# Gate rows by transposes in place of fp32 products with the identity: a hybrid pooling and attention backbone on one core

## The chip, the core and the metric

The kernel runs on one core of a Trainium2 chip. The engines that matter are TensorE (PE in the profile; PEld is its weight load), VectorE (DVE), ScalarE (ACT), GpSimd (POOL) and SyncE (SP), which issues the DMAs. TensorE multiplies a stationary operand, which is loaded first, with a moving operand, and writes the result to PSUM. A transpose on TensorE is an instruction of the same form with its transpose flag set, with the data as one operand and the identity as the other.

The metric is device time in microseconds. Three timed runs of the kernel before gave 1163.19 to 1163.43 us, median 1163.33 us. The execution that was profiled took 1161.48 us.

## The reference

Two layers work on 512 latent tokens and 256 context tokens of 1024 channels, in fp32. The first layer mixes tokens by pooling over windows, the second by attention, and each is followed by a squared-ReLU MLP. Each sub-layer is normalised, shifted and scaled before, and multiplied by a gate after:

```python
for i in range(DEPTH):
    sh1, sc1, gt1, sh2, sc2, gt2 = ada_mods(c, w_ada[i], b_ada[i])
    csh1, csc1, cgt1, csh2, csc2, cgt2 = ada_mods(c_ctx, w_ada[i], b_ada[i])
    h_lat = modulate(rms_norm(x, g_mix_pre[i]), sh1, sc1)
    h_ctx = modulate(rms_norm(ctx, g_mix_pre[i]), csh1, csc1)
    ...
    x = x + gt1 * rms_norm(y_lat, g_mix_post[i])
    ...
    x = x + gt2 * rms_norm(m_lat, g_mlp_post[i])
```

The gate has one value per channel, the product of `gt1` (or `gt2`) and the gain of the norm behind it. The context tokens have gates of their own (`cgt1`, `cgt2`) in the first layer.

## The kernel before

Tokens lie in six tiles of 128 rows (0 to 3 latent, 4 and 5 context). Large products run in fp32r: operands are split into a high and a low part, and three products (high with high, high with low, low with high) are summed in PSUM. ACT makes the high part, DVE the low one.

Conditioning: `ada_mm` multiplies the two conditioning vectors with weights that come by DMA in loads of 1 MB (tile `raw`, result `psada`). `ada_rows`, `ada_sel` and `ada_mods` turn the result into columns: channel k*128 + p lies in partition p, column k of `mods`. The shift and scale of a channel are used in that form.

The gate is needed as a row instead: it multiplies tiles with tokens in the partitions and channels along the free axis, and so has to stand in every partition. `gate_cols` (L317) makes the column form `gc` on DVE. `gate_half` (L326) makes 512 channels of the row form in a PSUM tile `psg`: for each of four columns of `gc` it takes the column, repeated 128 times by a zero stride, as the stationary operand and the identity as the moving one. The result has the column's 128 values along the free axis, the same in each partition. ACT then copies the tile to `gate` in SBUF, and DVE uses it in `gated` (L361). `gate_rows` (L334) calls `gate_half` twice and makes the copies; `gate_diag` (L341) is another way to the same rows, used at three other places, which the change doesn't touch.

`gate_half` runs in two places:

- First stage. Its steps are a list written by hand (`FIRST`), and the instructions of PE, DVE and ACT are kept in that order (class `Kept`; such instructions appear under line 87). The steps `psg:1:0`, `psg:0:0`, `psg:1:1` and `psg:0:1` are four calls (context and latent tokens, two halves of the channels). The copies are the steps `gate:`, the multiplies the steps `b:`, the residuals `r:`; between them stand the pooling products (`pool:`, tile `pspool`), the conditioning products for the MLP (`mm:SC2_0a` and on), their rows, selections and columns (`rows:`, `sel:`, `mods:`), and after them the transposes of the normalised rows (`turn:`, function `turn0`, tile `psx`) and the first products of the MLP (`in:`, tile `psin`).
- Attention. `gate_rows` for GT1 of layer 1 is given a due time between the last product of the probabilities with the values (`s_values`, L1378, tile `po`) and the output products (`attn_mm`, L1403, tile `psy`), whose results `gated` multiplies. The transposes of the probabilities are those of `s_turn` (L1359, tile `pspt`).

Outside the first stage the order is a planner's. Steps are sorted by due times; the framework then simulates the program (option `schedule_with_timeline_sim`) and orders each engine's instructions by that order and by when they are ready. Some instructions are pinned (`keep_in_program_order`). SP issues the DMAs in order; a load waits until its buffer is free.

The first MLP computes its inner products in rounds of seven chains of twelve products (`Seven.chain`, L732), between which ACT copies partial sums (L740, L744); `ada_sum` (L296 to L305) does the remaining conditioning on DVE meanwhile. After the attention output, `norm_pair`, `half_early` and `upper_half` (L1472) prepare the second MLP, whose first products are at L608.

Of the kernel before, what the change touches and what calls it, by code (L numbers as in the profile page):

```python
# [17 lines left out]
P = 128  # L18
# [72 lines left out]
def backbone(ctx: ExitStack, tc, x, ctx_in, w_ada, w_pool, pool_scale, w_qkv, g_q, g_k, w_o, w_mlp_in,  # L91
# [4 lines left out]
    te, ve, sc = Kept(tc, nc.tensor, ordered), Kept(tc, nc.vector, mixed), Kept(tc, nc.scalar, mixed)  # L96
# [20 lines left out]
    ident = const.tile([P, P], F32, name="ident")  # L117
# [208 lines left out]
    def gate_half(ci, h):  # L326
        ps = psB.tile([P, 512], F32, tag="b", name="psg")
        gc = halfgate.pop((ci, h))
        for k in range(4):
            te.matmul(ps[:, k * P:(k + 1) * P], gc[:, 4 * h + k:4 * h + k + 1].broadcast_to([P, P]), ident,  # L330
                      start=True, stop=True)
        halfgate[ci, h] = ps

    def gate_rows(i, m, ci):  # L334
        gc = gate_cols(i, m, ci)
        for h in range(2):
            halfgate[ci, h] = gc
            gate_half(ci, h)
            sc.copy(gate[:, ci, 512 * h:512 * h + 512], halfgate.pop((ci, h)))
# [80 lines left out]
    def mod0(t, q, on_act):  # L420
        ci, ps = 0 if t < NL else 1, turned[t, q]
        for kk in range(2):
            k = 2 * q + kk
            sa, b = avec[0][1][:, k, ci:ci + 1], mods[0][:, SH2 * KT + k, ci:ci + 1]
            h, src = accv[:, t:t + 2, k * P:(k + 1) * P], ps[:, kk, :].rearrange("p (u n) -> p u n", n=P)
            if on_act:
                sc.activation(h, src, AF.Identity, scale=sa, bias=b)
            else:
                ve.tensor_scalar(out=h, in0=src, scalar1=sa, scalar2=b, op0=ALU.mult, op1=ALU.add)
        ks = slice(2 * q, 2 * q + 2)  # L430
        h = accv[:, t:t + 2, 2 * q * P:(2 * q + 2) * P].rearrange("p u (k n) -> p k u n", n=P)
        turned[t, q] = (h, *(z.rearrange("p k (h q n) -> p k q h n", h=2, n=P)[:, ks, t // 2] for z in (hH, hL)))
# [380 lines left out]
    def halved(t, q, part):  # L813
        h, hi, lo = turned[t, q]
        if part:
            ve.tensor_tensor(out=lo, in0=h, in1=hi, op=ALU.subtract)
        else:
            sc.copy(hi, h)

    def keep(store, key, fn, *args):  # L820
        store[key] = fn(*args)
# [5 lines left out]
        sel=lambda x: conditioning(ada_sel, x), mods=lambda x: conditioning(ada_mods, x),  # L827
        hi=lambda k: centred(k, 0), lo=lambda k: centred(k, 1), pool=pool_a,
        gc=lambda ci, h: keep(halfgate, (ci, h), gate_cols, 0, GT1, ci, 4 * h, 4 * h + 4), psg=gate_half,
        gate=lambda ci, h: sc.copy(gate[:, ci, 512 * h:512 * h + 512], halfgate.pop((ci, h))),  # L830
        ms=pool_ms, rs=lambda t: keep(rs, t, rstd, rs[t], 2 if t in (4, 1) else 1),
# [5 lines left out]
        h=lambda t, act, q: mod0(t, q, act), xhi=lambda t, q: halved(t, q, 0), xlo=lambda t, q: halved(t, q, 1))  # L837
# [749 lines left out]
```

## Time and profile before

| | before |
|---|---|
| timed runs, median of 3 | 1163.33 us |
| profiled execution | 1161.48 us |
| its span, first to last instruction | 1159.7 us |
| PE busy, instructions | 1140.7 us (98%), 6172 |
| DVE busy | 932.7 us (80%) |
| ACT busy | 628.8 us (54%) |
| mean granted TensorE clock | 0.999 |

The span is 1.78 us shorter than the execution's time; the rest lies before the first and after the last instruction. Matmuls are pipelined, so that the time of one from start to end is longer than the distance between two; the chain of waits counts each only for the time that it holds up the next. In the chain a row gives start, length, engine, tile, line and count of instructions. In the timeline a bracket gives the idle time of the engine ahead of a group and what ended it.

### The profile page before, as it was taken

The numbers are of one execution on the slowest core, as the hardware profiler recorded it, in microseconds if no ns is written. First come the engines' busy times: TensorE is split into PE (matmuls) and PEld (weight loads), VectorE is DVE, ScalarE is ACT, GpSimd is POOL, SyncE is SP. The second block draws the span as 40 slices with busy tenths as digits, with TensorE's granted clock in tenths as the row PEclk, the third lists the DMA queues.
The fourth block names the chain that finished last, engine by engine and source line by source line (L and its number), as shares of the span: only waits on it lengthen the run. The fifth ranks groups of instructions, "written<-read, shape, count | busy, mean of one in ns | idle before, by whom it ended". The sixth has DMA issues, their size and how long they took to land.

```text
span 1159.7 us, 15945 instructions
## 1 busy us (share of the span) xinstructions
PE 1140.7 (98%) x6172; PEld 990.7 (85%) x6172; DVE 932.7 (80%) x1515; ACT 628.8 (54%) x1068; POOL 69.2 (6%) x120
## 2 busy tenths in 40 slices
PE   7999999999999999999999999999999999999997
PEld 5679889998898988998888889998988888888886
DVE  4688588998988997996777699867687679778876
ACT  5676555554354534555675367753676436534522
POOL 2130000000000000000242200001100000000001
PEclk9999999999999999999999999999999999999999
DMA  9964222443334444343422102125334214313212
GB/s 374 418 270 151 73 99 87 146 145 131 123 145 146 146 146 145 109 146 109 182 73 73 37 1 74 37 74 168 122 146 146 81 64 146 109 44 138 109 41 104
DMA packets 25516, 147.32 MB, mean 127 GB/s; under 512 B 2785, under 2 KB 5217, under 8 KB 9698
## 3 DMA queue, kind: packets, MB, share of 16 engines
q1 hardware_dynamic: 25442, 146.32, 34.4%
q8 instruction: 48, 0.79, 0.3%
q14 instruction: 26, 0.21, 0.1%
HBM read 138.96 MB, written 7.34 MB: 126 GB/s over the span
## 4 chain that ended last, share of the span: by engine, by line
PE 62%; issue 30%; DVE 2%; POOL 2%; ACT 2%; DMA 1%; POOLq 0%; SPq 0%; DVEq 0%; ACTq 0%
PE pso L878 22%; PE psin L732 18%; PE psy L1403 3%; PE po L1378 3%; PE pss L1337 3%; PE psq L1133 2%; PE pspt L1359 2%; PE pspool L87 2%; PE psin L87 1%; PE psin L608 1%; PE psada L87 1%; DMA raw<-in_w_ada 1%; PE psm L87 1%; POOL rs L211 1%; PE psg L87 1%
## 5 line engine op out<-in xcount | busy, mean ns | idle before, releaser
L878 PE MATMUL pso<-units,rb 128*128 128x512 f32 x1152 | 278.8, 392 | 0.0
L878 PEld LDWEIGHTS pso<-units,rb 128*128 128x128 f32 x1152 | 214.7, 188 | 41.1
L301 DVE SCALAR_TENSOR_TENSOR rows<-raw,cond,rows 128x256 f32<-128x256 f32 x280 | 127.2, 478 | 2.0
L890 DVE TENSOR_TENSOR acc<-acc,pso 128x512 f32<-128x512 f32 x129 | 85.4, 676 | 40.5 <-PE pso L878 40.3
L608 PE MATMUL psin<-ra,rb 128*128 128x512 f32 (+1 forms) x310 | 87.8, 360 | 0.0
L987 PE MATMUL pso<-units,pairs 128*128 128x512 f32 x336 | 82.6, 389 | 0.0
L608 PE MATMUL psin<-ra 128*128 128x512 f32 (+1 forms) x256 | 76.5, 376 | 0.0
L987 PEld LDWEIGHTS pso<-units,pairs 128*128 128x128 f32 x336 | 63.1, 188 | 13.1
L991 DVE TENSOR_TENSOR acc<-acc,pso 128x512 f32<-128x512 f32 x72 | 48.7, 682 | 26.2 <-PE pso L987 26.2
L732 PE MATMUL psin<-ra,units 128*128 128x384 f32 x336 | 65.6, 337 | 0.4 <-ACT psin L744 0.4
L209 POOL TENSOR_SCALAR ms<-ss 128x1 f32<-128x1 f32 x16 | 8.7, 541 | 936.6 <-ACT junk L196 922.9
L732 PE MATMUL psin<-sums,units 128*128 128x384 f32 x336 | 64.0, 336 | 0.0
L732 PEld LDWEIGHTS psin<-ra,units 128*128 128x128 f32 x336 | 59.9, 188 | 3.9 <-ACT psin L744 0.5
L608 PEld LDWEIGHTS psin<-ra,rb 128*128 128x128 f32 x310 | 55.6, 189 | 8.7
L169 DVE TENSOR_TENSOR units<-raw,units 128x1024 fp32r<-128x1024 f32 (+2 forms) x49 | 55.1, 1152 | 8.6 <-ACT units L166 8.4
L732 PEld LDWEIGHTS psin<-sums,units 128*128 128x128 f32 x336 | 58.9, 188 | 1.6
L608 PE MATMUL psin<-rb 128*128 128x512 f32 (+1 forms) x155 | 55.8, 361 | 0.6 <-DVE rb L1472 0.6
L166 ACT CAST units<-raw 128x1024 fp32r<-128x1024 f32 (+2 forms) x49 | 46.9, 996 | 17.0 <-PE pso L878 12.9
L608 PEld LDWEIGHTS psin<-ra 128*128 128x128 f32 x256 | 47.1, 188 | 8.8
L888 ACT COPY acc<-pso 128x512 f32<-128x512 f32 x48 | 27.1, 586 | 46.9 <-PE pso L878 46.4
L1133 PE MATMUL psq<-units,ra 128*128 128x512 f32 x216 | 52.2, 393 | 0.0
L608 PE MATMUL psin<-rb,ra 128*128 128x512 f32 (+1 forms) x128 | 48.1, 376 | 0.0
(284 smaller groups left out, 2385.5 us busy)
## 6 DMA issues: line engine op xcount, KB each, us to landing
raw<-in_w_ada SPq DMA_DIRECT2D x48, 1024.0 KB, 5.2
raw<-in_w_mlp_in SPq DMA_DIRECT2D x32, 1024.0 KB, 4.9
raw<-in_w_mlp_out SPq DMA_DIRECT2D x32, 1024.0 KB, 5.8
raw<-in_w_qkv SPq DMA_DIRECT2D x6, 1024.0 KB, 4.9
spill<-xr SPq DMA_DIRECT2D x10, 512.0 KB, 4.3
xr<-spill SPq DMA_DIRECT2D x10, 512.0 KB, 6.7
raw<-in_w_o SPq DMA_DIRECT2D x4, 1024.0 KB, 4.8
xr<-in_x SPq DMA_DIRECT2D x4, 512.0 KB, 5.3
```

The source lines that it names most:

```text
L87: return lambda *args, **kw: self.tc.keep_in_program_order(f(*args, **kw))
L166: a = sc.copy(hi, raw)
L169: b = ve.tensor_tensor(out=lo, in0=raw, in1=hi, op=ALU.subtract)
L301: ve.scalar_tensor_tensor(out=r, in0=raw[:, k, :], scalar=cond[:, k, c:c + 1], in1=r, op0=ALU.mult, op1=ALU.add)
L608: te.matmul(ps[:, bank, o:o + ln], w[:, k, fs], rhs, start=start, stop=(k == KT - 1 and n == 2), skip_group_check=len(ks) < KT or self.paired)
L732: te.matmul(bank, w[k], a[k], start=start and k == 0 and m == 0, stop=stop and k == 3 and m == 2, skip_group_check=True)
L878: te.matmul(pss[h][:, 0:cols[h][1]], a[:, f, ts_], w[:, f, cols[h][0]:sum(cols[h])], start=(n == 0 and not seeded[t]), stop=(n == len(seq) ...
L890: ve.tensor_tensor(out=d, in0=d, in1=ps[:, 0:w], op=ALU.add)
L987: te.matmul(ps, a, w, start=(m == 0), stop=(m == len(seq) - 1))
L991: ve.tensor_tensor(out=M[n][:, t], in0=M[n][:, t], in1=ps, op=ALU.add)
L1133: te.matmul(ps, a[:, k, sl], w[:, k % 4, :], start=(k == 0 and n == 0), stop=(k == KT - 1 and n == 2))
L1337: te.matmul(ps[:, c2, 0:384], a[:, sl], b[:, kv, 384 * c2:384 * c2 + 384], start=(n == 0), stop=(n == 2))
```

## The change

`gate_half` calls the transpose in place of the product; operands, tile, count of calls and what waits for them stay as they are.

```diff
         ps = psB.tile([P, 512], F32, tag="b", name="psg")
         gc = halfgate.pop((ci, h))
         for k in range(4):
-            te.matmul(ps[:, k * P:(k + 1) * P], gc[:, 4 * h + k:4 * h + k + 1].broadcast_to([P, P]), ident,
-                      start=True, stop=True)
+            te.transpose(ps[:, k * P:(k + 1) * P], gc[:, 4 * h + k:4 * h + k + 1].broadcast_to([P, P]), ident)
         halfgate[ci, h] = ps
```

## The prediction

> **What bounds the kernel.** I read the page first, then the chain of waits around the two places where gate rows are made, then what each engine waited for there.
>
> ```profile
> span 1159.7 us, 15945 instructions
> PE 1140.7 (98%) x6172; PEld 990.7 (85%) x6172; DVE 932.7 (80%) x1515; ACT 628.8 (54%) x1068; POOL 69.2 (6%) x120
> PEclk9999999999999999999999999999999999999999
> ```
>
> TensorE (PE) is busy for 1140.7 of 1159.7 us at full clock, so work that leaves PE is worth its time if nothing else ends last in its stage. That has to be seen stage by stage. The chain through the first place (start, length, what):
>
> ```profile
> 46.64 0.91 PE pspool L87 x6
> 47.55 0.89 PE psg L87 x8
> 48.44 1.00 PE psada L87 x8
> 49.44 1.09 PE psg L87 x8
> ...
> 52.32 0.89 PE psg L87 x8
> 53.21 0.71 PE pspool L87 x6
> 53.93 0.89 PE psg L87 x8
> ...
> 67.45 0.87 PE psx L87 x8
> 68.33 0.22 PE psada L87 x13
> ```
>
> and a window over the same stretch (length, busy time of each engine, clock, DMA share, GB/s):
>
> ```profile
> 47.39:68.55 21.16, 21.16 (x190) 15.91 (x188) 14.08 (x18) 15.44 (x28) 9.41 (x16) 1.00 1.01 418
> ```
>
> Between 47.4 and 68.5 us the chain lies on PE without a break: 21.16 us busy of 21.16. The four gate halves (psg) stand in that chain, so PE ends last there. DMA is full as well (share 1.01), and has to be examined below. The second place, in the attention:
>
> ```profile
> 769.57 0.22 PE psg L330 x2
> 769.79 1.07 PE po L1378 x9
> 770.86 1.56 PE psg L330 x14
> 772.42 38.12 PE psy L1403 x168
> ```
>
> Again PE goes from the last value products (po) through psg into 38 us of output products (psy) with no gap.
>
> **What one half costs now and then.** A half is four products of 128x128, one per 128 channels.
>
> ```profile
> L87 PE MATMUL psg<-ident,gc x32: 270/275/376, 47.4 to 54.5; 128*128 128x128 f32 x32
> L330 PE MATMUL psg<-ident,gc x16: 270/275/275, 769.4 to 772.1; 128*128 128x128 f32 x16
> ```
>
> Sixteen calls of the first stage leave 32 records and eight calls of the attention leave 16: a full fp32 product is two passes. The 275 ns is a latency; what a call takes of the pipe is read from the chain: 0.89 / 8 = 0.111 us per pass. One half shows 1.09 instead of 0.89; the 0.20 more is its start behind the narrow psada products, and I leave it in place. Transposes in this kernel, timeline and then chain:
>
> ```profile
> 86.10 1.91 PE L87 MATMUL psx<-ident,acc 128*128 128x128 f32 x16
> ```
>
> ```profile
> 72.98 1.02 PE psx L87 x8
> ...
> 86.26 1.75 PE psx L87 x16
> ```
>
> Sixteen calls (one group of turn0 is four calls, and four groups run here) leave sixteen records: a fp32 transpose is one pass, of 1.75 / 16 = 0.109 us. Where a group starts behind psada, as in the row at 72.98, it is 1.02 / 8 = 0.128 with the start included.
>
> **The sum.** Before: 0.89 + 1.09 + 0.89 + 0.89 = 3.76 us in the first stage and 0.22 + 1.56 = 1.78 us in the attention, 5.54 in all. After: 16 x 0.109 + 0.20 = 1.94 and 8 x 0.109 = 0.87, 2.81 in all. Gain 1.82 + 0.91 = 2.73 us.
>
> No row has a transpose whose data operand repeats one column (zero stride), so its price is bounded. From below by 0.109, since no transpose row is faster; from above by 2 x 0.111 = 0.222, what the same operand costs in the full product, at which the gain is nothing. With 0.128 for all 24 the gain is 5.54 - 3.07 = 2.47. I take 0.109, since the present psg passes, with the same repeated column, keep 0.111 against 0.109 and so show no sign that the stride matters. Nothing is added elsewhere: same tiles, same PSUM buffers, same copies to the gate, no DMA, no new wait.
>
> The Trainium skill, page "TensorE: Matmul & The Clock Gate", section "Terms", calls the transpose mode four times faster for FP32. By that a half would be 0.89 / 4 = 0.22 us and the gain 4.0 us, an estimate from that page. The trace has one record in place of two and 0.109 against 0.111 per record, so a factor of two; the sum goes by the trace.
>
> **What is late next, first stage.** The instructions of that stage keep the order of the list FIRST on PE, DVE and ACT, so nothing is reordered there; PE's steps after the fourth half come 1.8 us earlier if their inputs do. Three streams could hold them back.
>
> DMA: eight loads of conditioning weights go out from 34.67 us on, in the order SC2_0a, SC2_0b, SH2_0a and so on. The second, issued at 37.41, is the tightest:
>
> ```profile
> 37.41 0.33 SPq L147 DMA_DIRECT2D raw<-in_w_ada  x1
> ```
>
> ```profile
> raw<-in_w_ada SPq DMA_DIRECT2D x1, 1024.0 KB, 16.5
> ```
>
> ```profile
> 55.46 1.07 PE L87 MATMUL psada<-raw,cond 128*32 128x512 f32 x8
> ...
> 57.36 1.06 PE L87 MATMUL psada<-raw,cond 128*32 128x512 f32 x8
> ```
>
> It lands at 37.41 + 16.5 = 53.9 and is used at 57.36, so there are 3.4 us, and 1.6 remain after a shift of 1.8. DMA is full but ahead.
>
> ACT and DVE, and a window over DVE's longest run (DVE is the third busy time):
>
> ```profile
> 53.25 0.59 ACT L87 COPY gate<-psg 128x512 f32<-128x512 f32 x1 [1.16 <-PE psg L87]
> ...
> 69.11 1.02 ACT L87 ACTIVATE acc<-psx,mods,avec 128x256 f32<-128x256 f32 x2 [2.61 <-DVE mods L87]
> ```
>
> ```profile
> 53.87 1.23 DVE L87 TENSOR_TENSOR acc<-acc,gate 128x1024 f32<-128x1024 f32 x1 [0.21 <-ACT gate L87]
> ...
> 65.17 0.72 DVE L87 STREAM_TRANSPOSE work<-psada 128x512 f32<-128x512 f32 x1 [0.96 <-PE psada L87]
> 68.57 0.17 DVE L87 TENSOR_TENSOR mods<-psada,vec 128x8 f32<-128x8 f32 x1 [2.68 <-PE psada L87]
> ```
>
> ```profile
> 53.87:64.22 10.35, 10.35 (x85) 7.27 (x87) 9.93 (x10) 8.75 (x16) 6.85 (x10) 1.00 1.01 419
> ```
>
> DVE is busy for 9.93 of the 10.35 us from 53.87 to 64.22, the rest being the steps between instructions, and that run starts when the third half's gate copy ends. The copy can come 3 x 0.45 us earlier, but DVE's own work in front of the run ended only 0.21 us before it and moves by the two halves ahead of it, 0.9: the run moves by 0.9 + 0.2 = 1.1 us, not 1.8. The missing 0.7 us is covered: DVE waits for PE 0.96 us at 65.17 and 2.68 us at 68.57, and ACT waits 2.61 us at 69.11. With that idle gone the price would be 0.7. So the whole 1.8 us arrives at 68.5, where DVE and ACT start the next stage from PE's result, and everything behind, its DMAs included, moves by the same amount.
>
> **Attention.** The eight calls stand between po and psy. The gate copies that follow (ACT) serve the multiply at 778.0, which waits for psy anyway. Later waits:
>
> ```profile
> 778.01 0.69 DVE L361 TENSOR_TENSOR acc<-psy,gate 128x512 f32<-128x512 f32 x1 [0.49 <-PE psy L1403]
> ...
> 810.58 0.69 DVE L361 TENSOR_TENSOR acc<-psy,gate 128x512 f32<-128x512 f32 x1 [1.74 <-PE psy L1403]
> ```
>
> ```profile
> 822.84 0.39 PE L608 MATMUL psin<-rb 128*128 128x256 f32 x1 [0.61 <-DVE rb L1472]
> ```
>
> At 778 DVE has 0.49 us of idle, less than 0.91, so its filler work moves less than PE; by 810.58 it has 1.74 us in hand, and that covers it. PE's only wait there, 0.61 us for the lower half's split, hangs on DVE and ACT steps that start from the last psy product, and moves along. If DVE's cover were gone, 0.4 us of the 0.91 would be.
>
> **Forecast.** Profiled execution: 1161.48 us, span 1159.70 and 1.78 around it. Span after 1159.70 - 2.73 = 1156.97, that execution 1158.75. The median of the timed runs is 1.85 us above the profiled one; the same 2.73 off it gives 1163.33 - 2.73 = 1160.6 us, a gain of 0.23%. What a measurement can tell from no change is 0.2%, 2.33 us, so this clears it by 0.4 us only.
>
> **Rivals.**
>
> 1. Half is hidden. Another stream takes over in the first stage and only the attention's 0.91 counts: 1162.4. For it: DMA at 1.01 and DVE without idle for ten microseconds. Against: 1.6 us of slack on the tightest load, 2.68 us of DVE idle before 68.57.
>
> 2. A new plan makes it slower. Outside the first stage most instructions are not pinned; their order comes from a planner that simulates the program, and a shorter psg can change it. Place: the products of the first MLP (L732) and the copy of their partial sum (L744), behind the changed stage. PE waited for that copy once (the 0.4 behind the last bar):
>
> ```profile
> L732 PE MATMUL psin<-ra,units 128*128 128x384 f32 x336 | 65.6, 337 | 0.4 <-ACT psin L744 0.4
> ```
>
> A round has two such chains of twelve, so the 336 records are fourteen rounds. If ACT ran a cast ahead of that copy in every round, 14 x 0.4 = 5.6 us are lost and 2.73 gained: 1166.2. It decides from seven rounds on (2.73 / 0.4). For it: the same loop body is planned anew each round, and ACT has casts ready beside the copy. Against: behind 68.5 us all streams move alike, so the planner sees the same relative times there. A smaller slip, one to six rounds, only eats into the gain: 1161 to 1163.
>
> 3. The repeated column makes the transpose slow, above 0.222 us a call. At four passes, 0.436, a half takes 1.74: 24 x 0.436 + 0.20 = 10.7 in place of 5.5, 1168.5. Against: no transpose row shows it.
>
> 4. With the repeated column the transposes run at half of 0.109, a quarter of the present two passes: 24 x 0.055 + 0.20 = 1.5 in place of 5.54, 1159.3. Against: 0.109 us in the transpose rows. The rule of the Trainium skill cited above would give this time.
>
> 5. The clock falls. Transposes run four or eight in a row, and if they did not count as activity PE might go on at half clock. From 47.39 to 55.46 that doubles 8.07 us: 1160.6 + 8.1 = 1168.7. Against, the window over sixteen transposes in a row:
>
> ```profile
> 86.10:87.85 1.75, 1.75 (x19) 1.75 (x18) 1.69 (x4) 1.24 (x3) 0.00 (x0) 1.00 1.14 323
> ```
>
> The clock stays at 1.00. The Trainium skill, same page, section "Part 4: PE-mode transpose", says that transposes are not counted as PE busy in the same way; this trace shows no loss from it.
>
> 6. It does not do what it says: the call still becomes two passes. Then nothing changes, 1163.3; the sixteen psx records for sixteen calls speak against it.
>
> **Chances.** Forecast 0.65 (1160.2 to 1161.2); rival 1, with small slips of rival 2, 0.17; rival 2 in full 0.09; rival 3 0.03; rival 4 0.03; rival 5 0.01; rival 6 0.02. Faster by over 0.2% means under 1161.0: most of the forecast's own range (0.57 of 0.65) and rival 4, 0.60. Slower by over 0.2%, above 1165.7: rivals 2 (in full), 3 and 5, 0.13. The rest, 0.27, is within. The range runs from rival 4's side, 1159.4, to 1163.6, above rival 6; it leaves out rival 4 and the slower cases, 0.16.
>
> **What would show it.** In the changed profile psg has 16 records in the first stage and 8 in the attention, near 272 ns, and 0.44 us a half in the chain; the step of SC2's mods (68.57) comes at 66.8 with DVE idle in front of it; psy starts at 769.7 (both gains); PE's busy time is 2.7 us lower and its idle time the same. A psg wait on another engine, a load that PE waits for between 53 and 68, or a longer idle at L732 or at L608 after psy would show the forecast wrong.

## The result and the profile after

Over eleven runs of each, taken on one chip, the changed kernel has a median of 1159.48 us (1159.24 to 1161.62) and the kernel before 1163.19 us (1161.78 to 1164.28); the ratio is 0.9972, 95% interval 0.9964 to 0.9981, so 2.2 to 4.2 us were gained. The prediction was 1160.6 us, with a range of 1159.4 to 1163.6. The profiled execution took 1159.78 us.

The page of the changed kernel (span; busy time, share and instructions of each engine; granted clock):

```profile
span 1158.0 us, 15894 instructions
...
PE 1139.0 (98%) x6148; PEld 988.4 (85%) x6148; DVE 932.4 (81%) x1515; ACT 629.0 (54%) x1068; POOL 71.0 (6%) x120
...
PEclk9999999999999999999999999999999999999999
```

24 matmul records are gone, as the change says. But PE is busy only 1.7 us less, and the span is shorter by only 1.7, where 2.7 were counted. Where the missing microsecond lies is seen by cutting at the first psg. Windows of the kernel before: up to its first psg, and from there to its first psx:

```profile
0.00:47.39 47.39, 38.66 (x337) 27.29 (x337) 26.98 (x59) 28.28 (x44) 7.46 (x18) 1.00 0.97 392
47.39:67.29 19.90, 19.90 (x166) 14.90 (x165) 14.08 (x18) 15.44 (x28) 9.41 (x16) 1.00 1.01 418
```

The same two windows of the changed kernel:

```profile
0.00:48.43 48.43, 39.67 (x336) 27.90 (x337) 26.89 (x59) 28.28 (x44) 7.58 (x18) 1.00 0.96 389
48.43:66.47 18.04, 18.04 (x150) 12.99 (x149) 13.99 (x18) 15.53 (x28) 10.38 (x16) 1.00 1.01 419
```

This execution reached the first psg 1.04 us later, with 1.01 us more PE busy time ahead of it, in work that the change doesn't touch. From the first psg to the first psx it took 18.04 us in place of 19.90, busy throughout in both, with 16 records fewer. So absolute times of two profiles are not compared here, but stretches that begin at the first psg.

The chain of the changed kernel in the first stage, and in the attention:

```profile
48.59 0.44 PE psg L87 x4
...
50.02 0.58 PE psg L87 x4
...
52.40 0.44 PE psg L87 x4
...
53.55 0.44 PE psg L87 x4
```

```profile
768.69 0.11 PE psg L330
...
769.04 0.11 PE psg L330
...
769.98 0.66 PE psg L330 x6
770.63 4.57 PE psy L1402 x20
```

A half is 0.44 us, or 0.58 behind psada, in place of 0.89 and 1.09. The sums are 1.90 in place of 3.76 us, and 0.88 in place of 1.78. The instructions of the tile psg (count: shortest, median and longest ns, first and last start) have the same latency and half the count:

```profile
L87 PE MATMUL psg<-ident,gc x16: 270/272/322, 48.4 to 53.7; 128*128 128x128 f32 x16
...
L330 PE MATMUL psg<-ident,gc x8: 271/272/273, 768.5 to 770.4; 128*128 128x128 f32 x8
```

What DVE waited for, in the timeline of the changed kernel:

```profile
53.66 1.22 DVE L87 TENSOR_TENSOR acc<-acc,gate 128x1024 f32<-128x1024 f32 x1
...
64.35 0.72 DVE L87 STREAM_TRANSPOSE work<-psada 128x512 f32<-128x512 f32 x1 [0.35 <-PE psada L87]
67.75 0.17 DVE L87 TENSOR_TENSOR mods<-psada,vec 128x8 f32<-128x8 f32 x1 [2.68 <-PE psada L87]
...
808.79 0.69 DVE L360 TENSOR_TENSOR acc<-psy,gate 128x512 f32<-128x512 f32 x1 [1.77 <-PE psy L1402]
```

DVE's idle at the first psada row fell from 0.96 to 0.35 us, while the 2.68 us ahead of the last mods stayed. PE's groups with idle time show nothing new (busy us, mean ns, idle us ahead and what ended it):

```profile
L731 PE MATMUL psin<-ra,units 128*128 128x384 f32 x336 | 65.6, 337 | 0.4 <-ACT psin L743 0.4
...
L607 PE MATMUL psin<-rb 128*128 128x512 f32 (+1 forms) x155 | 55.9, 362 | 0.6 <-DVE rb L1471 0.6
```

One thing did move that was not in the sum. In the attention output the planner put the reduce L305, which frees the buffer of the second MLP's first load, behind the second gate multiply on DVE. In the timeline before, and then after:

```profile
782.21 0.42 DVE L305 TENSOR_REDUCE part<-raw 128x8 f32<-128x256 f32 x1
783.38 0.69 DVE L361 TENSOR_TENSOR acc<-psy,gate 128x512 f32<-128x512 f32 x1 [0.75 <-PE psy L1403]
```

```profile
781.59 0.69 DVE L360 TENSOR_TENSOR acc<-psy,gate 128x512 f32<-128x512 f32 x1 [0.75 <-PE psy L1402]
782.19 0.41 DVE L305 TENSOR_REDUCE part<-raw 128x8 f32<-128x256 f32 x1
```

The load goes out 12.24 us behind the first psy where it was 10.48.

### The profile page after: what moved, and what is told of

The parts are those of the page before. It is cut to its first block, busy times and chain, and to the rows that moved or that the text cites. A ratio compares the mean times of both kernels' runs of the same rounds, so it can differ in the third digit from the quotient of the medians.

```text
span 1158.0 us, 15894 instructions
## 1 busy us (share of the span) xinstructions
PE 1139.0 (98%) x6148; PEld 988.4 (85%) x6148; DVE 932.4 (81%) x1515; ACT 629.0 (54%) x1068; POOL 71.0 (6%) x120
## 3 DMA queue, kind: packets, MB, share of 16 engines
HBM read 138.96 MB, written 7.34 MB: 126 GB/s over the span
## 4 chain that ended last, share of the span: by engine, by line
PE 62%; issue 30%; DVE 2%; POOL 2%; ACT 2%; DMA 2%; SPq 0%; POOLq 0%; DVEq 0%; ACTq 0%
PE pso L877 22%; PE psin L731 18%; PE psy L1402 3%; PE po L1377 3%; PE pss L1336 3%; PE psq L1132 2%; PE pspt L1358 2%; PE pspool L87 2%; PE psin L87 1%; PE psin L607 1%; PE psada L87 1%; DMA raw<-in_w_ada 1%; POOL rs L211 1%; PE psm L87 1%; POOL rs L1141 1%
## 5 line engine op out<-in xcount | busy, mean ns | idle before, releaser
L877 PEld LDWEIGHTS pso<-units,rb 128*128 128x128 f32 x1152 | 214.7, 188 | 41.1
```

The costliest lines, as they stand in the source:

```text
L877: te.matmul(pss[h][:, 0:cols[h][1]], a[:, f, ts_], w[:, f, cols[h][0]:sum(cols[h])], start=(n == 0 and not seeded[t]), stop=(n == len(seq) ...
```

## The experiments

Two theories stood at the start: the whole gain is the halved passes, at places where PE ends last (2.73 us by the prediction); or part of the 3.7 us between the medians has another source, such as the new plan. Five stretches of each profile tell where time is won or lost (us):

| run | first psg at | psg to psx | psx to the attention's psg | psg to psy | psy to second MLP's psin | psin to end |
|---|---|---|---|---|---|---|
| before | 47.39 | 19.90 | 702.12 | 2.77 | 45.68 | 341.84 |
| after | 48.43 | 18.04 | 702.06 | 1.86 | 45.68 | 341.94 |
| e0, same | 50.11 | 19.90 | 702.10 | 2.77 | 45.68 | 341.84 |
| e1, first stage | 48.35 | 18.04 | 702.10 | 2.77 | 45.68 | 341.85 |
| e2, attention | 49.15 | 19.90 | 702.11 | 1.86 | 46.85 | 341.91 |
| e3, both | 49.15 | 18.04 | 702.13 | 1.86 | 45.68 | 341.90 |
| e4, twice | 48.79 | 19.78 | 702.06 | 2.73 | 45.68 | 341.86 |
| e5, shared | 50.31 | 17.21 | 702.12 | 1.86 | 45.68 | 341.91 |
| e6, no diagonals | 51.22 | 18.04 | 712.13 | 1.87 | 46.17 | 344.65 |
| e7, pinned | 48.71 | 18.04 | 702.11 | 1.86 | 45.68 | 342.04 |
| e8, slow load | 48.11 | 18.04 | 702.09 | 1.86 | 45.69 | 341.80 |
| e9, pinned and slow | 50.19 | 18.04 | 702.09 | 1.86 | 45.68 | 341.97 |
| e10, no diagonals, padded | 49.24 | 18.04 | 705.75 | 1.86 | 45.68 | 341.89 |
| e11, 32 bytes moved | 48.17 | 18.04 | 706.99 | 1.86 | 46.17 | 345.17 |

**The kernel before again** (e0), unchanged.

> The kernel before, unchanged, against itself. It gives what the measurement makes of no change, and a second profile of before: theory (the 1.06 us by which the changed kernel's profile is late at 47.5 us comes from the first loads, not from the change) expects the time at which the first psada product of GT1 starts to differ by up to 1 us between two profiles of the same program, and a ratio of 1.000 within 0.001.

Ratio 1.0001 (0.9992 to 1.0010). Its profile is 2.7 us longer than the first one of the same kernel, all of it ahead of the first psg: the start differs that much between executions, and by more than the 1 us that was expected.

**One place at a time** (e1 and e2).

```diff
-            te.transpose(ps[:, k * P:(k + 1) * P], gc[:, 4 * h + k:4 * h + k + 1].broadcast_to([P, P]), ident)
+            col = gc[:, 4 * h + k:4 * h + k + 1].broadcast_to([P, P])
+            if ordered[0]:
+                te.transpose(ps[:, k * P:(k + 1) * P], col, ident)
+            else:
+                te.matmul(ps[:, k * P:(k + 1) * P], col, ident, start=True, stop=True)
```

In e2 the condition is reversed.

> Transposes in the four halves of the first stage alone, products in the attention. Theory (PE ends last there): 1.82 us less, ratio 0.9984. Rival (half is hidden behind DMA or DVE): 0 to 0.9 us less. In the profile the stretch from the first psg to the first psx is 1.82 us shorter by the theory.

> Transposes in the two halves of the attention alone. Theory: 0.91 us less, ratio 0.9992, with the stretch up to the first psg of the attention as before. Rival (the excess of the measured gain over 2.73 us comes from a new order behind the attention): 1.5 to 2 us less.

e1: 1160.91 us, ratio 0.9986 (0.9977 to 0.9994). e2: 1162.32 us, ratio 1.0000 (0.9991 to 1.0009), which holds 0.91 us of gain and none. The stretches tell more than the times: each place gives its own part, 1.86 and 0.91 us, and nothing at the other. e2 also has the new place of the reduce, and there one stretch grew from 45.68 to 46.85 us. Its timeline:

```profile
792.61 1.91 ACT L166 CAST rb<-raw 128x2048 fp32r<-128x2048 f32 x1 [6.89 <-DMA raw<-in_w_mlp_in]
...
794.55 2.29 DVE L169 TENSOR_TENSOR rb<-raw,rb 128x2048 fp32r<-128x2048 f32 x1 [3.32 <-ACT rb L166]
...
813.61 1.75 PE L388 MATMUL psx<-ident,acc 128*128 128x128 f32 x14 [0.94 <-ACT acc L563]
```

The load took 7.32 us to land where it took 4.90 in the changed kernel's profile. ACT and DVE, which both wait for it in order, were late by it, and PE waited 0.94 us at psx. In the kernel before the same load also took 7.34 us, but went out 1.76 us earlier, and PE lost nothing. So the new plan gives away slack on this load. On DVE, ACT and GpSimd the order of e2 is the changed kernel's, instruction by instruction, so an execution of the changed kernel with a load as slow would be expected to lose as much; none of its profiles has one. That the load cost the 1.17 us is read from the waits of this one execution.

**Both places again** (e3), the changed kernel itself.

> The changed kernel again, on the same chip as the parts. Theory: the sum of the two parts, 2.73 us less, ratio 0.9977; the 3.3 to 3.7 us seen at first are partly differences between runs. Rival (something outside the two places gains too): 3.3 us or more again, ratio 0.9972 or less, and more than the two parts together.

1160.43 us, ratio 0.9980 (0.9971 to 0.9989), beside 0.9972 the first time. Both intervals hold 2.77 us (0.9976). The 3.7 us of the first comparison are therefore no sign of a second gain.

**The transposes twice** (e4).

```diff
-            te.transpose(ps[:, k * P:(k + 1) * P], gc[...].broadcast_to([P, P]), ident)
+            for _ in range(2):
+                te.transpose(ps[:, k * P:(k + 1) * P], gc[...].broadcast_to([P, P]), ident)
```

> The changed kernel with each of the 24 transposes issued twice into the same place, so the cost of the transposes alone is put back on TensorE and nothing else changes on the other engines. Theory (PE ends last in both places, every transpose pass of 0.109 us counts in full): the first stage's stretch from the first psg to the first psx, 18.04 us in the changed kernel, becomes 18.04 + 16 x 0.109 = 19.78 us; the attention's stretch from the first psg to the first psy, 1.86 us, becomes 1.86 + 8 x 0.109 = 2.73 us; the time is 2.6 us above that of the changed kernel, ratio to the kernel before 1.000 within 0.001. Rival (a stream other than PE has taken over in the first stage, so that the last part of the halves was hidden): the first stretch grows by less than 1.74 us, the floor under it shows as PE idle. Rival (the stretch got shorter for another reason than the passes, such as the rearranged copies): the stretches stay below 19.0 and 2.3 us.

The stretches are 19.78 and 2.73 us, to the hundredth as expected, and the time is 1162.84 us, ratio 1.0001 (0.9992 to 1.0010). Its chain shows a half at the price of before with transposes alone:

```profile
48.95 0.87 PE psg L87 x8
...
50.82 1.02 PE psg L87 x8
```

So every pass counts in full, and the gain is passes and nothing else.

**Two halves fewer in the first stage** (e5).

```diff
+        if ordered[0] and ci == 0:
+            halfgate.pop((ci, h))
+            halfgate[ci, h] = shared[h]
+            return
...
+        shared[h] = ps
```

> The changed kernel with the gate rows of the latent tokens of the first stage left out: the two psg tiles of the context are copied for both, so two of the four halves and their eight transposes are not computed (this part of the result is left out). It asks how much more could be had where the four halves stand. Theory (PE still ends last there): the stretch from the first psg to the first psx falls from 18.04 to 17.2 us, 8 x 0.109 = 0.87 less, with DVE's idle ahead of the last mods still over 1 us. Rival (the DVE run of ten microseconds behind the gate copies has become the end): the stretch stays within 0.3 us of 18.04 and PE shows new idle in it. Time 0.9 us under the changed kernel at most, not to be told by one look.

The kernel leaves out the latent tokens' own gate rows of this stage, and it ran once (1160.86 us), so only the stretch is read: 17.21 us. In this execution nothing else has become the end there even after 2.7 us less PE work than in the kernel before, and DVE is still idle ahead of the last mods:

```profile
68.80 0.17 DVE L87 TENSOR_TENSOR mods<-psada,vec 128x8 f32<-128x8 f32 x1 [2.60 <-PE psada L87]
```

**The other gates as well** (e6), a try at a faster kernel.

```diff
     def gate_diag(i, m, ci, to=None):
-        to = ci if to is None else to
-        gc = gate_cols(i, m, ci)
...
-            sc.copy(gate[:, to, 512 * h:512 * h + 512], ps)
+        gate_rows(i, m, ci)
```

> The changed kernel with the three remaining gates (L340, one vector spread to rows by products of ones with two diagonal tiles, 4 products of 128x512 in fp32r and two 128x1024 multiplies on DVE per gate) also made by transposes of the repeated column. PE per gate: now 4 x 0.222 = 0.89 us, then 8 x 0.109 = 0.87; DVE per gate 2 x 1.22 + 0.33 = 2.8 us less, 8.3 in all. Theory (a gain comes only where passes leave PE, and here none leave): the time is that of the changed kernel within 0.5 us, ratio to the kernel before 0.997 to 0.9985; PE busy within 0.3 us, DVE busy 8 us lower. Rival (DVE is near the bound around 550 us, where PE waited 0.4 us for a diagonal): up to 0.4 us faster than the changed kernel. Rival (the planner orders the work around 550 us anew): a stage elsewhere moves by more than 1 us, either way.

1173.41 us, ratio 1.0094 (1.0079 to 1.0109): 11 us slower than the kernel before, which neither the theory nor the 0.4 us rival allowed. DVE is 5.3 us less busy (8 were expected), but PE 12.8 us more, with only twelve records more. Part of it is what the last rival named, a new order: at the handover from the first MLP to the next layer PE now waits. A window over it in the changed kernel and in e6:

```profile
590.00:602.00 12.00, 12.00 (x61) 10.14 (x60) 11.70 (x19) 8.54 (x20) 8.18 (x6) 1.00 0.50 169
```

```profile
590.00:602.00 12.00, 10.08 (x57) 7.92 (x55) 11.05 (x18) 10.58 (x22) 3.63 (x5) 1.00 0.00 0
```

The rest, which no rival named, was spread over the whole kernel: products of pso came every 230.6 ns on average in place of 227.1. Two runs below take that up.

**The reduce put back** (e7).

```diff
-            gated(t, y1[:, t, :], ps, c0, c0 + width)
+            z = gated(t, y1[:, t, :], ps, c0, c0 + width)
+            if (ch, t) == (0, 1):
+                tc.keep_in_program_order(z)
```

> The changed kernel with one gate multiply of the attention (the one of the second psy tile, L360) pinned to program order, which puts the reduce of the first ada_sum (L305) ahead of it on DVE again as in the kernel before; the buffer of the load for the second MLP comes free 1.3 us earlier. Theory (the gain is the 24 halved transposes, and the new place of the reduce only uses up slack on this load): both stretches as in the changed kernel, 18.04 and 1.86 us; the load is issued about 10.9 us behind the first psy in place of 12.2; first psy to first psin of the second MLP 45.68 us; the median equal to the changed kernel's or up to 0.5 us under it, ratio to the kernel before 0.996 to 0.998. Rival (the new place costs in most executions, so that the attention's 0.91 us are lost in them): the median 0.9 to 1.2 us under the changed kernel's, ratio 0.9965 or less.

1160.51 us, ratio 0.9983 (0.9974 to 0.9992); the load goes out 10.93 us behind psy. The time is that of the changed kernel (1159.48 and 1160.43 us, ratios 0.9972 and 0.9980), and the rival's 0.9965 or less lies outside the interval, so the new place doesn't cost in most executions.

**A slower load** (e8 with the new place of the reduce, e9 with the old).

```diff
+        if slow[0]:
+            sy.dma_start(t[:, 0:128], src[:, 0:128])
         d = sy.dma_start(t, src)
...
+        at(19.99, slow.__setitem__, 0, True)
...
+        at(20.01, slow.__setitem__, 0, False)
```

> The changed kernel with a small extra load of 128 columns into the same tile just ahead of the second MLP's first weight load (the one whose buffer the reduce L305 frees), so that the weights land later. In the runs so far the first psin of the second MLP comes 45.68 us behind the first psy, except in the run with the attention's transposes alone, where the load was issued 12.24 us behind psy, landed 7.32 us later, at 19.56, and PE lost 1.17 us. Theory (PE starts to wait when the load lands later than 19.56 - 1.17 = 18.39 us behind psy; the new place of the reduce leaves it 18.39 - 12.24 = 6.15 us): the stretch is 45.68 + (landing - 18.39) us, about 46.9 if the extra load costs two microseconds. Rival (the 1.17 us had another cause): 45.68 within 0.1 us although the load lands behind 18.6. The planner sees the extra load and places some DVE steps of this stretch anew, so a stall must be traced to the load by its wait.

> The kernel with the pinned gate multiply (reduce L305 ahead of it again) and the same small extra load ahead of the second MLP's first weight load. Theory: the load is issued about 10.9 us behind the first psy and so may take up to 18.39 - 10.9 = 7.5 us; landing 7.3 us later or less costs nothing, first psy to first psin 45.68 us within 0.1; beyond it only the excess. Rival (the stall does not hang on when the buffer comes free): as much stall as in the same kernel without the pin.

Each ran once (1159.41 and 1161.66 us), so only the stretches are read. In e8 the load landed 19.16 us behind psy (issued at 14.19, 4.97 to land), which by the theory costs 0.77 us; the stretch is 45.69 us, so nothing. The number missed. The planner had seen the longer load and placed a square of psy on ACT and a residual on DVE ahead of its users:

```profile
789.34 1.91 ACT L168 CAST rb<-raw 128x2048 fp32r<-128x2048 f32 x1 [1.06 <-DMA raw<-in_w_mlp_in]
...
791.28 2.29 DVE L171 TENSOR_TENSOR rb<-raw,rb 128x2048 fp32r<-128x2048 f32 x1 [0.36 <-ACT rb L168]
```

ACT waited 1.06 us there instead of 6.89. What a late load costs thus hangs on the order of the steps around it as well. Since e8 has an order of its own, it is no test of the 1.17 us, which belong to the order that e2 and the changed kernel share. e9 has no stall, as expected, but its load landed at 17.70, inside the slack of either order, so it tells nothing apart.

**Addresses** (e10 and e11). e10 is e6 with an unused tile as large as the one that e6 doesn't need; its order is e6's. e11 is the changed kernel with one small tile ahead of `units` 32 bytes a partition shorter; its order is the changed kernel's.

```diff
     halfgate = {}
+    small.tile([P, 2, KT], F32R, tag="gh", name="gh", bufs=2)
```

```diff
-    phase = ctx.enter_context(tc.tile_pool(name="phase", bufs=1)).tile([P, 40], F32, name="phase")
+    phase = ctx.enter_context(tc.tile_pool(name="phase", bufs=1)).tile([P, 32], F32, name="phase")
```

> The kernel without diagonal tiles again, with one unused tile of two 64-byte buffers in the place of those that it no longer needs, so that every tile behind it lies at the address that it had in the changed kernel; the order on every engine is that of the kernel without diagonal tiles. There the products that take units as an operand came every 232 ns in place of 227, and PE lost 2.7 us once around 591 us. Theory (the 128 bytes moved the units tile and that made its products slow): pso products from units back at 227 ns, mean pitch 227.1 against 230.6, time 5 to 8 us below that of the kernel without diagonal tiles, 1165 to 1168, ratio to the kernel before 1.002 to 1.005, the rest being the wait at 591. Rival (the new order is what slows them, through more traffic on the memory at the same time): pitch stays at 230 or more and the time within 1 us of 1173.4.

> The changed kernel with the small tile phase, which lies ahead of the units tile, 32 bytes shorter (40 numbers a partition in place of 32 used); the order on every engine is exactly that of the changed kernel, only addresses behind it move by 32 bytes. Theory (the address of units sets the pitch of its products): the pitch of the pso products moves away from 227 ns or stays, and where it moves only products with units as an operand do; with 232 ns the time is 6 to 9 us longer, ratio to the kernel before 1.002 to 1.005. Rival (the address plays no part): pitch 227.1 and the changed kernel's time, ratio 0.997 to 0.998.

e10: 1164.34 us, ratio 1.0018 (1.0008 to 1.0027), pitch of pso (from one start to the next) 227.1 ns. So 9.1 us of e6's time went with the 128 bytes, more than the 5 to 8 that were expected, and the time lies just below the expected 1165 to 1168. e6's profile also has a second fall of the clock, to 0.50 from 604.27 us on for 3.41 us, which e10's lacks; what share it has in the 9.1 was not separated. The remaining loss against the changed kernel is the wait of the new order, 3.63 us in this window of e10:

```profile
590.00:602.00 12.00, 8.37 (x42) 6.19 (x41) 11.55 (x20) 10.53 (x24) 5.59 (x6) 1.00 0.39 127
```

e11: 1168.33 us, ratio 1.0052 (1.0037 to 1.0067), pitch of pso 230.5 ns: some 8 us lost by 32 bytes, with no instruction added or moved. The same two groups of products, in the changed kernel and in e11:

```profile
L986 PE MATMUL pso<-units,pairs x336: 389/389/389, 858.4 to 1115.0; 128*128 128x512 f32 x168
...
L986 PE MATMUL pso<-ra,pairs x168: 389/389/389, 843.7 to 1092.5; 128*128 128x512 f32 x168
```

```profile
L986 PE MATMUL pso<-units,pairs x336: 392/396/398, 863.6 to 1122.9; 128*128 128x512 f32 x168
...
L986 PE MATMUL pso<-ra,pairs x168: 389/389/389, 848.9 to 1100.1; 128*128 128x512 f32 x168
```

Of these two groups only the one that streams `units` got longer. No version tried is faster than the changed kernel.

## Why the prediction was right

**The sum.** Predicted 1.82 us in the first stage and 0.91 in the attention, 2.73. Measured by the stretches 1.86 and 0.91, 2.77. The 0.04 are, within the rounding, the start behind psada, left in place at 0.20 and measured at 0.58 - 0.44 = 0.14. Each place alone (e1, e2) gave its own term, and doubling the passes took both back (e4).

**The price of a transpose of a repeated column.** Taken at 0.109 us between bounds of 0.109 and 0.222; measured 0.44 / 4 = 0.11. The repeated column costs nothing and saves nothing, and 24 records are gone: rivals 3, 4 and 6 fall. The rule behind rival 4, of the Trainium skill (page "TensorE: Matmul & The Clock Gate", section "Terms"), gave 0.22 us a half. The trace doesn't agree: 0.44, a factor of two against the full product.

**Cover in the first stage.** DVE's long run was to move by 1.1 us, not 1.8. Counted from the first psg it moved from 53.87 - 47.39 = 6.48 to 53.66 - 48.43 = 5.23, by 1.25, and the missing part came out of DVE's idle at psada (0.96 to 0.35). The last mods still wait 2.68 us for PE, so all of it arrived. Rival 1 falls; e5 shows, in one execution, that another 0.83 us arrives too. The load that the prediction called the tightest was issued at 38.38, took 16.2 us and was used at 56.53, so 1.9 us remained, where 1.6 were counted.

**The attention.** DVE's idle at the later gate multiply is 1.77 us, where it was 1.74, and PE's 0.6 us ahead of the second MLP is still there and moved along, as the two stretches of 45.68 us show.

**The plan.** Rival 2 named the first MLP as the place where the planner could slip; PE's idle there is the same 0.4 us in all. Its chance was put where nothing happened. What was not foreseen is the exchange of two DVE steps in the attention output. It hangs on the shorter psg of the attention: the load goes out 12.24 us behind psy in the changed kernel, e2, e3, e5, e6 and e10, and 10.48 in the kernel before, e0, e1 and e4, where those transposes are absent or doubled. It costs nothing in the changed kernel's profiles (45.68 us), and e2, which has the same exchange, lost 1.17 us in the one execution whose load was slow.

**The clock.** It stayed at 1.00 over the whole stretch with the transposes, so rival 5 falls, and what the Trainium skill says of transposes and the clock (same page, section "Part 4: PE-mode transpose") costs nothing here, where at most six of the new ones stand in a row between products.

**The median.** 1160.6 was predicted; the same kernel gave 1159.48 in one set of runs and 1160.43 in another. The first lies below the forecast's own 1160.2 to 1161.2 and next to rival 4's 1159.3, and only 0.08 us inside the whole range, which is luck: it is the stretches that bear the forecast out, not this time. The size was carried over from the profile to the median with its start unchanged, and the start varies by more than the gain: the first psg lies between 47.39 and 51.22 us in the fourteen profiles. Part of the spread goes with the clock: of the eleven executions of the changed kernel, the eight with a mean granted clock of 0.999 took 1159.24 to 1159.78 us, the three with 0.995 to 0.997 took 1160.26 to 1161.62. The step from profile to median was the uncertain one, not the sum. For the same reason the prediction's own sign, PE busy 2.7 us lower, reads 1.7: 2.75 less behind the first psg, 1.01 more ahead of it.

## What to carry to other kernels

Where a full fp32 product with the identity only moves data, a transpose does it in half the passes, and the gain is the passes times the pitch read from the chain, wherever PE ends last and the engines behind it have idle time left. Where the alternative already has as few passes (the diagonal tiles here: by estimate 0.89 us a gate against 0.87, and PE is busy for 1139.0 us in the changed kernel and in e10 alike), nothing is to be had from PE, and an edit that frees memory can cost far more by moving the tiles behind it. Measure an edit of a few microseconds by stretches between two of its own instructions, since the start of the kernel varies by as much.

## What the runs showed of the hardware

**32 bytes, 8 us.** Products of 512 columns that stream `units` came every 226.7 ns (pso from units and pairs) in the changed kernel, every 232.1 with that tile 128 bytes lower (e6) and every 233.2 with it 32 bytes lower (e11); with the 128 bytes put back it was 226.7 again (e10). Products from `ra`, which didn't move, kept 226.7 in all four. Which addresses are good, and why, was not tried.

**The clock at the start.** In six of the fourteen profiles the granted clock fell to 0.50 once between 31.7 and 41.1 us, for 3.41 us (e0, e2, e9 and e11) or 6.83 us (e5 and e6), in none of the others. PE waits for conditioning weights there. The recorded changes of the clock within a profile lie whole multiples of 3.41 us apart, in all fourteen. So each profile can be cut into steps of 3.41 us counted from these changes. The step ahead of the fall and the fall, in e0 and in e5 (PE's busy time follows the length, the clock is the third figure from the end):

```profile
31.51:34.92 3.41, 1.32 (x24) 0.66 (x24) 2.76 (x10) 2.91 (x5) 0.00 (x0) 1.00 1.01 420
34.92:38.33 3.41, 3.26 (x30) 2.46 (x31) 2.77 (x8) 2.54 (x5) 0.00 (x0) 0.50 1.02 423
```

```profile
28.69:32.10 3.41, 1.71 (x36) 0.97 (x32) 1.55 (x5) 0.20 (x1) 0.00 (x0) 1.00 1.01 420
32.10:38.93 6.83, 5.89 (x49) 3.83 (x50) 5.53 (x13) 5.93 (x11) 0.00 (x0) 0.50 1.02 423
```

In the kernel before, PE was idle as long as in e0 in one stretch of 3.41 us (the first line), but two of its steps share that stretch (the other lines), and the clock stayed:

```profile
30.10:33.51 3.41, 1.32 (x24) 0.66 (x24) 2.76 (x10) 3.02 (x5) 0.00 (x0) 1.00 1.01 423
```

```profile
27.49:30.90 3.41, 2.00 (x40) 0.97 (x32) 1.71 (x6) 0.67 (x2) 0.00 (x0) 1.00 1.02 423
30.90:34.31 3.41, 1.83 (x32) 1.11 (x36) 2.97 (x6) 3.41 (x7) 0.00 (x0) 1.00 1.01 420
```

PE was idle for 1.63 to 2.10 us in the step ahead of each of these six falls and of e6's second one, and for 2.03 us or more in the step ahead of the fall that ends each profile. Of all other steps only two reach 1.6 us, and the clock stayed behind them: 1.63 in e3 and 1.77 in the changed kernel, from 1149.49 us on. So the fall goes with PE's idle time in one such step, and the same waits fall into one step in some executions and into two in others. That is an agreement over fourteen profiles, with no sharp bound, and no run tested it. The Trainium skill (same page, section "Part 1: The HAM clock gate") has the clock fall after an idle window of about 3.4 us; no single gap of PE between 20 and 40 us was longer than 1.43 us in these profiles, so that this alone doesn't explain it. Where the clock fell, the first psg came at 48.17 to 51.22 us, elsewhere at 47.39 to 49.24.

**One load, three durations.** The same 1 MB load behind psy landed 4.72 to 5.11 us after its issue in seven profiles, 6.13 to 6.18 in three, and 7.32 and 7.34 in two (e8 and e9, whose load follows another, are left out). The cause was not tried.
